# Splitting the mixers' and output projections' fp32 weights into high and low parts in four pieces instead of one or two

## The chip, the core and the metric

The kernel runs on one core of a Trainium2 chip. The metric is the device time of one execution in microseconds. The kernel is profiled once beside the timed runs; every row below is from that one execution.

## What is computed

The reference is one inference step of a two-layer streaming encoder for a prompt of 1024 tokens and a sample chunk of 64 tokens that share all weights. Model width is 1024, the feed-forward width 2816.

```
h = rmsnorm(x, norm_g[l, 0]) * (1.0 + sc1) + sh1
layer 0: retention (4 heads) || differential attention (4 heads):  h @ w_in_ab ... concat @ w_out_ab
layer 1: band attention (8 heads) || Mamba-2 SSD (8 heads):        h @ w_in_cd ... concat @ w_out_cd
x = x + g1 * out
h = rmsnorm(x, norm_g[l, 1]) * (1.0 + sc2) + sh2
u = h @ w_up[l]; a, g = u[:2816], u[2816:]
x = x + g2 * ((a * gelu(causal_dwconv(g))) @ w_down[l])
```

sc, sh and g come from the conditioning vector c (`silu(c) @ w_mod + b_mod`). The output is the final norm of x and all new caches and states, in fp32.

## The kernel before

All matrix products of the trunk are made in fp32r from two operands each: a high part `hi` (a copy rounded to fp32r) and a low part `lo = raw - hi`. A product is three matmuls: hi·hi, hi·lo and lo·hi. Activations are stored features-by-tokens in three token chunks of 384 columns (the third has 320), each as a hi and a lo tile.

**Weights.** A weight group is 256 output columns of a projection for all eight 128-row blocks k of the contraction, so a tile of 128 x 2048 fp32. `load_raw` (L185) or `load_two_raw` (L914) issues its DMA from SyncE's queue into `raw`, a pool of two buffers. `split_w` (L191) then takes `whi` and `wlo`, pools of two buffers each, and splits: ScalarE casts `raw` to `whi` (L198), and GpSimd (in the page's terms POOL) subtracts `whi` from `raw` into `wlo` (L199). The whole tile is one cast and one subtraction, unless the caller sets `urgent`: then there are two halves, the first subtracted by VectorE (DVE), the second by POOL. `urgent` is set in three places: the first query-key group of layer 0 (L1078), the first B/C group of layer 1 (L1706) and the first z group of layer 1 (L1783). 40 tiles go through `split_w`: the projections of the mixers (`load_two`, `load_cols`), the two output projections (L491, L1628, L2165) and the last pair of `w_down` rows of each layer (`load_rows`, L206). The up projection and most of `w_down` have a splitter of their own, `split` (L594, its cast is L595, its subtraction L596), which always works in pieces of 512 or 544 columns.

**Stages.** Layer 0 begins with the modulation and the first norm, then retention head by head (`core_ret`), with the projections of the next head woven between (`proj_ret`); then differential attention head by head (`diff_attention`), again with the next head's projection as filler; then the output projection, the feed-forward's up part in a Strassen-like form (`ffn_up`, L648) and its down part (`ffn_down`, L804). Layer 1 begins inside the end of `ffn_down` (`to_layer1`), goes through `project_z`, `project_x` and the state-space scan (`scan_group`) and band attention (`band_attention`), and ends as layer 0 does.

**What sets the order.** The five engines each run their own instruction list in order. The program is written as Python generators that are woven together, and a scheduler of the framework then orders each engine's list once more when the kernel is built. So an edit of one helper can shift neighbouring instructions of all engines.

Names that the prediction uses: `post` is the convolved SSD projection and `tt` its tanh, multiplied into it by DVE at L160 (`stt` is a helper, so all its calls have the line L160); `zt` is the gated z; `st` the SSD state, scaled on POOL (L1934) and added to on DVE (L1935); `t` stands for scan work tiles, which DVE subtracts `cum` from at L1911; `qj` holds attention queries as hi and lo parts (L1358); `pt` is the transposed probabilities; `cf` a row's factor in differential attention; `dg` a diagonal for the norm; `macc` the modulation's sums.

Of the kernel before, what the change touches and what calls it, by code (L numbers as in the profile page):

```python
# [142 lines left out]
def build(ctx, tc, A, O, stop=None):  # L143
    nc = tc.nc
    V, S, G, T = nc.vector, nc.scalar, nc.gpsimd, nc.tensor
# [45 lines left out]
    def split_w(raw, sz, urgent=False):  # L191
        hi = wsp.tile([P, WU], F32R, tag="whi", name="whi")
        lo = wsp.tile([P, WU], F32R, tag="wlo", name="wlo")
        n = 2 if urgent else 1
        for i in range(n):
            eng = V if urgent and i == 0 else G
            sl = slice(sz * i // n, sz * (i + 1) // n)
            S.copy(hi[:, sl], raw[:, sl])  # L198
            eng.tensor_tensor(out=lo[:, sl], in0=raw[:, sl], in1=hi[:, sl].bitcast(F32), op=ALU.subtract)  # L199
        return hi, lo  # L200

    def load_cols(w, c0, n=256, urgent=False):
        hi, lo = split_w(load_raw(w_src(w, c0, n), KT, n), KT * n, urgent)
        return [t[:, :KT * n].rearrange("p (k n) -> p k n", n=n) for t in (hi, lo)]

    def load_rows(w, r0):  # L206
        src = w[r0:r0 + 256, :].rearrange("(k p) n -> p k n", p=P)
        hi, lo = split_w(load_raw(src, 2, D), 2 * D)
        return [t[:, :2 * D].rearrange("p (k n) -> p k n", n=D) for t in (hi, lo)]
# [714 lines left out]
    def split_two(raw, urgent=False):  # L924
        hi, lo = split_w(raw, 2048, urgent)
        return [t[:, :2048].rearrange("p (k n) -> p k n", n=256) for t in (hi, lo)]
# [792 lines left out]
    class Modulation:  # L1719

        gen, n, every = None, 0, 1
# [517 lines left out]
```

## Time and profile before

| what | value |
|---|---|
| median of 3 runs | 2973.62 us (2972.55 to 2975.34) |
| the profiled execution's own time | 2973.83 us |
| its span, first to last instruction | 2972.1 us |
| mean granted TensorE clock | 0.979 of full speed |
| PE busy | 2804.1 us, 94% of the span |
| DVE busy | 1954.3 us, 66% |
| ACT busy | 1296.3 us, 44% |
| POOL busy | 787.3 us, 26% |

PE is TensorE's matmuls, ACT is ScalarE. An engine counts as busy from the start of an instruction to its end, also while the instruction stands still because something else holds what it needs; DVE's share must be read with that in mind. Windows of the page show PE at nine tenths or more in the feed-forward stages, and at seven or eight tenths in the start, late in each attention part, and where layer 1 begins.

### The profile page before, as it was taken

The numbers are of one execution on the slowest core, as the hardware profiler recorded it, in microseconds if no ns is written. First come the engines' busy times: TensorE is split into PE (matmuls) and PEld (weight loads), VectorE is DVE, ScalarE is ACT, GpSimd is POOL, SyncE is SP. The second block draws the span as 40 slices with busy tenths as digits, with TensorE's granted clock in tenths as the row PEclk, the third lists the DMA queues.
The fourth block names the chain that finished last, engine by engine and source line by source line (L and its number), as shares of the span: only waits on it lengthen the run. The fifth ranks groups of instructions, "written<-read, shape, count | busy, mean of one in ns | idle before, by whom it ended". The sixth has DMA issues, their size and how long they took to land.

```text
span 2972.1 us, 51195 instructions
## 1 busy us (share of the span) xinstructions
PE 2804.1 (94%) x19418; PEld 2707.4 (91%) x19418; DVE 1954.3 (66%) x4095; ACT 1296.3 (44%) x2938; POOL 787.3 (26%) x842
## 2 busy tenths in 40 slices
PE   7999999889999999999988999997999999999998
PEld 4999998779899999999988998986998999999997
DVE  5788766654788666587876675456268888764544
ACT  4221265644535444555552335556255454334111
POOL 4332222222255444412342352111100000004131
PEclk9999999889999999999989999999999999999999
DMA  7444421135544333553422331113344533235221
GB/s 241 139 131 142 126 62 60 46 98 159 158 130 137 91 101 96 183 173 128 138 82 74 86 98 50 52 55 93 99 132 144 153 101 102 71 98 184 90 81 61
DMA packets 351069, 330.53 MB, mean 111 GB/s; under 512 B 24898, under 2 KB 307047, under 8 KB 350823
## 3 DMA queue, kind: packets, MB, share of 16 engines
q1 hardware_dynamic: 350823, 327.26, 35.7%
q8 instruction: 153, 2.51, 0.4%
q14 instruction: 93, 0.76, 0.1%
HBM read 248.46 MB, written 78.73 MB: 110 GB/s over the span
## 4 chain that ended last, share of the span: by engine, by line
PE 47%; DVE 9%; DMA 6%; ACT 4%; issue 2%; POOL 1%; SPq 0%; DVEq 0%; ACTq 0%; POOLq 0%
PE dps L804 10%; PE pa L648 7%; PE pe L648 6%; PE pb L648 6%; DMA mh<-in_w_mod 3%; PE py L648 3%; PE qkps L231 3%; PE pvps L2110 2%; DMA raw<-in_w_up 2%; DVE macc L455 1%; ACT mh L453 1%; PE ops L231 1%; PE xps L231 1%; DVE wlo L596 1%; PE ptps L1316 1%
## 5 line engine op out<-in xcount | busy, mean ns | idle before, releaser
L804 PE MATMUL dps<-y,whi 128*128 128x384 f32 (+1 forms) x2112 | 518.8, 330 | 5.9 <-DVE sthi L160 4.2
L804 PEld LDWEIGHTS dps<-y,whi 128*128 128x128 f32 x2112 | 376.0, 189 | 7.2 <-DVE sthi L160 4.7
L595 ACT CAST whi<-raw 128x512 fp32r<-128x512 f32 x328 | 194.7, 617 | 372.4 <-PE pb L648 95.0
L804 PE MATMUL dps<-y,wlo 128*128 128x384 f32 (+1 forms) x1056 | 347.1, 330 | 0.0
L199 POOL TENSOR_TENSOR wlo<-raw,whi 128x2048 fp32r<-128x2048 f32 (+2 forms) x40 | 180.7, 4518 | 373.5 <-ACT whi L198 290.3
L160 DVE SCALAR_TENSOR_TENSOR x<-dps,modT,x 128x384 f32<-128x384 f32 (+1 forms) x320 | 149.4, 495 | 110.7 <-PE dps L804 110.1
L596 POOL TENSOR_TENSOR wlo<-raw,whi 128x512 fp32r<-128x512 f32 x116 | 162.1, 1402 | 208.1 <-ACT whi L595 203.1
L648 PE MATMUL pe<-row,whi 128*128 128x272 f32 x1056 | 205.9, 288 | 0.0
L804 PEld LDWEIGHTS dps<-y,wlo 128*128 128x128 f32 x1056 | 199.7, 189 | 0.0
L596 POOL TENSOR_TENSOR y<-y 128x544 fp32r<-128x544 f32 x88 | 133.0, 1543 | 250.4 <-ACT y L595 250.4
L453 ACT ACTIVATE mh<-mh,cact 128x256 f32<-128x256 f32 x336 | 145.8, 498 | 120.9 <-DMA mh<-in_w_mod 105.8
L455 DVE TENSOR_TENSOR macc<-macc,mh 128x512 f32<-128x512 f32 x168 | 142.7, 849 | 76.9 <-ACT mh L453 64.9
L596 DVE TENSOR_TENSOR wlo<-raw,whi 128x512 fp32r<-128x512 f32 x212 | 148.4, 718 | 64.1 <-ACT whi L595 63.4
L648 PE MATMUL pa<-row,whi 128*128 128x272 f32 x896 | 174.7, 292 | 10.3 <-ACT gs L669 10.3
L231 PE MATMUL qkps<-hhi,whi 128*128 128x384 f32 (+1 forms) x528 | 178.6, 342 | 3.3 <-DVE q L1383 2.0
L231 PE MATMUL qkps<-hlo,whi 128*128 128x384 f32 (+1 forms) x528 | 173.5, 332 | 0.0
L648 PEld LDWEIGHTS pe<-row,whi 128*128 128x128 f32 x1056 | 165.9, 188 | 0.0
L648 PE MATMUL pb<-bt,whi 128*128 128x272 f32 x816 | 156.8, 288 | 1.1 <-DVE u L717 1.1
L648 PE MATMUL pa<-bt,whi 128*128 128x272 f32 x768 | 151.0, 292 | 5.0 <-DVE row L160 3.1
L648 PEld LDWEIGHTS pa<-row,whi 128*128 128x128 f32 x896 | 143.1, 192 | 11.0 <-ACT gs L669 11.0
L648 PE MATMUL pe<-row,wlo 128*128 128x272 f32 x528 | 152.4, 289 | 0.0
L648 PE MATMUL py<-bt,whi 128*128 128x272 f32 x704 | 136.1, 290 | 4.0 <-ACT whi L595 2.4
(462 smaller groups left out, 8077.2 us busy)
## 6 DMA issues: line engine op xcount, KB each, us to landing
raw<-in_w_up SPq DMA_DIRECT2D x104, 512.0 KB
mh<-in_w_mod SPq DMA_DIRECT2D x96, 256.0 KB
yd<-e SPq DMA_DIRECT2D x88, 272.0 KB
y<-yd SPq DMA_DIRECT2D x44, 544.0 KB
raw<-in_w_down SPq DMA_DIRECT2D x22, 1024.0 KB
mq<-in_w_mod SPq DMA_DIRECT2D x64, 256.0 KB
raw<-in_w_in_ab SPq DMA_DIRECT2D x24, 512.0 KB
xr<-xspill SPq DMA_DIRECT2D x32, 193.0 KB
```

Of the source, the lines that this page charges most:

```text
L160: V.scalar_tensor_tensor(out=out, in0=in0, scalar=scalar, in1=in1, op0=op0, op1=op1, **kw)
L199: eng.tensor_tensor(out=lo[:, sl], in0=raw[:, sl], in1=hi[:, sl].bitcast(F32), op=ALU.subtract)
L231: T.matmul(out=ps[:, b:n], lhsT=lt, rhs=rh, start=(i == 0), stop=(i == len(mms) - 1))
L453: S.activation(out=pr[:, s, :], in_=rv[:, j - j0, :], func=AF.Copy, scale=cact[:, j, s:s + 1])
L455: V.tensor_add(acc, acc, pr)
L595: S.copy(hi, src)
L596: eng.tensor_tensor(out=lo, in0=src, in1=hi.bitcast(F32), op=ALU.subtract)
L648: T.matmul(out=ps[t], lhsT=lt, rhs=rh, start=(first and i == 0), stop=(i == len(mms) - 1), skip_group_check=not first)
L804: T.matmul(out=ps[:, :n], lhsT=lt, rhs=rh, start=(i == 0), stop=(i == len(mms) - 1))
L1316: T.transpose(ps[:kk, P * (b - b0):P * (b - b0 + 1)], e[:, P * b:P * b + kk], ident)
L2110: T.matmul(out=ps[:, :P], lhsT=pts[m][:kk, b, :], rhs=vv[:kk, :], start=(b == 0), stop=(b == nb - 1))
```

## The change

`split_w` works in four pieces, always: a 2048-column tile becomes four casts of 512 columns on ACT and four subtractions of 512 columns on POOL, piece by piece. With `urgent`, DVE subtracts the first two pieces and POOL the last two, so the columns of each of the two engines stay what they were. The z group has 2112 columns, so pieces of 528.

```diff
     def split_w(raw, sz, urgent=False):
         hi = wsp.tile([P, WU], F32R, tag="whi", name="whi")
         lo = wsp.tile([P, WU], F32R, tag="wlo", name="wlo")
-        n = 2 if urgent else 1
+        n = 4
         for i in range(n):
-            eng = V if urgent and i == 0 else G
+            eng = V if urgent and i < 2 else G
             sl = slice(sz * i // n, sz * (i + 1) // n)
             S.copy(hi[:, sl], raw[:, sl])
             eng.tensor_tensor(out=lo[:, sl], in0=raw[:, sl], in1=hi[:, sl].bitcast(F32), op=ALU.subtract)
```

Neither the number of matmuls nor a DMA changes. The scheduler's order does, in places. Two of them matter below.

The first is DVE at the start of layer 1, in `project_x`, where the tanh `tt` is multiplied into `post` while a z weight tile is split. Before:

```order
1834 L160 SCALAR_TENSOR_TENSOR post<-tt,post 128x384
1835 L160 SCALAR_TENSOR_TENSOR post<-acc_16682,pT_83,post 128x383
1836 L160 SCALAR_TENSOR_TENSOR post<-hist,pT_83,post 128x1
1837 L1858 COPY hist<-acc_16682 128x1
1838 L160 SCALAR_TENSOR_TENSOR post<-tt,post 128x384
1839 L160 SCALAR_TENSOR_TENSOR post<-acc_16683,pT_83,post 128x256
1840 L160 SCALAR_TENSOR_TENSOR post<-tt,post 128x384
1841 L160 SCALAR_TENSOR_TENSOR post<-acc_16683,pT_83,post 128x256
1842 L1791 TENSOR_TENSOR dtt<-zps,dtb 128x8
```

With the change:

```order
1846 L160 SCALAR_TENSOR_TENSOR post<-hist,pT_83,post 128x1
1847 L1858 COPY hist<-acc_16810 128x1
1848 L160 SCALAR_TENSOR_TENSOR post<-tt,post 128x384
1849 L160 SCALAR_TENSOR_TENSOR post<-acc_16811,pT_83,post 128x256
1850 L160 SCALAR_TENSOR_TENSOR post<-tt,post 128x384
1851 L1791 TENSOR_TENSOR dtt<-zps,dtb 128x8
1852 L160 SCALAR_TENSOR_TENSOR post<-acc_16811,pT_83,post 128x256
1853 L160 SCALAR_TENSOR_TENSOR post<-tt,post 128x384
```

The first of the three `tt` multiplications has moved down to the other two, because on ACT its tanh now stands behind the four casts.

The second is POOL late in the second half of the scan (`scan_group`), around the split of a weight group of band attention. Before:

```order
524 L1907 TENSOR_TENSOR t_18911<-t_18911,wl 128x256
525 L1943 TENSOR_TENSOR t_18824<-t_18824,t_18823 128x256
526 L1947 TENSOR_TENSOR t_18823<-t_18823 128x256
527 L1934 TENSOR_TENSOR st<-st,elast 128x256
528 L199 TENSOR_TENSOR wlo<-raw,whi 128x2048
529 L1950 TENSOR_SCALAR ss<-ss 128x1
```

With the change:

```order
528 L1907 TENSOR_TENSOR t_19073<-t_19073,wl 128x256
529 L199 TENSOR_TENSOR wlo<-raw,whi 128x512 x2
530 L1943 TENSOR_TENSOR t_18986<-t_18986,t_18985 128x256
531 L199 TENSOR_TENSOR wlo<-raw,whi 128x512 x2
532 L1934 TENSOR_TENSOR st<-st,elast 128x256
533 L1947 TENSOR_TENSOR t_18985<-t_18985 128x256
```

The state's scaling (L1934) stood ahead of the split and now stands behind all four pieces.

## Rows read from the trace of the kernel before

**Rows 1.** The page: busy time of the engines, and the chain that ended last by engine

```profile
PE 2804.1 (94%) x19418; PEld 2707.4 (91%) x19418; DVE 1954.3 (66%) x4095; ACT 1296.3 (44%) x2938; POOL 787.3 (26%) x842
...
PE 47%; DVE 9%; DMA 6%; ACT 4%; issue 2%; POOL 1%; SPq 0%; DVEq 0%; ACTq 0%; POOLq 0%
```

**Rows 2.** Who waited for line L198, the cast (us, times)

```profile
  PEld acc L216: 0.4, 1
```

**Rows 3.** Timeline at layer 1's start, POOL, DVE, PE (start us, us, what, idle)

```profile
1559.70 4.61 POOL L199 TENSOR_TENSOR wlo<-raw,whi 128x2048 fp32r<-128x2048 f32 x1 [6.92 <-ACT whi L198]
...
1560.08 4.64 DVE L160 SCALAR_TENSOR_TENSOR post<-tt,post 128x384 f32<-128x384 f32 x1 [2.73 <-ACT tt L1866]
...
1565.04 0.54 DVE L160 SCALAR_TENSOR_TENSOR post<-tt,post 128x384 f32<-128x384 f32 x1
...
1567.76 0.36 PE L247 MATMUL zps<-whi,hhi 128*128 128x264 f32 x1 [3.08 <-DVE zt L160]
```

**Rows 4.** Timeline of PE: idle behind other L199 splits, first group (last column: idle)

```profile
70.55 0.22 PE L1018 MATMUL mpt<-ident,mrow 2*128 2x2 f32 x1 [1.43 <-DVE mrow L1015]
...
100.52 0.39 PE L239 MATMUL vgps<-whi,hhi 128*128 128x256 f32 x1 [1.48 <-DVE rt L1172]
...
515.85 0.48 PE L1364 MATMUL sps<-ks,qj 128*128 128x512 f32 x1 [1.20 <-DVE mx L1304]
...
1664.27 0.36 PE L247 MATMUL zps<-whi,hhi 128*128 128x256 f32 x1 [1.24 <-DVE dco L1862]
```

**Rows 5.** The same, second group, with the DVE instruction that stood still

```profile
561.52 2.09 DVE L160 SCALAR_TENSOR_TENSOR cf<-sums,nlam,rr 128x1 f32<-128x1 f32 x1
...
565.71 0.50 PE L1364 MATMUL sps<-kcv,qj 128*128 128x512 f32 x1 [2.58 <-DVE kcv L1324]
...
1620.14 3.87 DVE L160 SCALAR_TENSOR_TENSOR post<-tt,post 128x320 f32<-128x320 f32 x1
...
1625.98 0.41 PE L231 MATMUL xps<-hhi,whi 128*128 128x386 f32 x1 [3.38 <-DVE post L1860]
...
2013.02 4.27 DVE L1358 TENSOR_TENSOR qj<-q,qj 64x128 fp32r<-64x128 f32 x1
...
2018.06 1.21 PE L2110 MATMUL pvps<-v,pt 128*128 128x128 f32 x8 [3.61 <-DVE pt L1318]
```

**Rows 6.** Groups by line and shape, POOL and ACT (busy us, mean ns; idle before)

```profile
L199 POOL TENSOR_TENSOR wlo<-raw,whi 128x2048 fp32r<-128x2048 f32 x37 | 172.5, 4663 | 372.7 <-ACT whi L198 289.6 <-PE ptps L1316 42.6 <-DVE x L160 16.6
L596 POOL TENSOR_TENSOR wlo<-raw,whi 128x512 fp32r<-128x512 f32 x116 | 162.1, 1402 | 208.1 <-ACT whi L595 203.1 <-DVE u L712 3.4 <-PE pe L648 1.5
...
L595 ACT CAST whi<-raw 128x512 fp32r<-128x512 f32 x328 | 194.7, 617 | 372.4 <-PE pb L648 95.0 <-PE dps L804 76.1 <-PE pa L648 62.9
...
L198 ACT CAST whi<-raw 128x2048 fp32r<-128x2048 f32 x37 | 70.6, 1908 | 106.4 <-PE dps L804 40.8 <-PE ops L217 30.8 <-issue 19.3
```

**Rows 7.** Timeline in layer 0's up projection, POOL and DVE, pieces of 512

```profile
830.10 1.27 POOL L596 TENSOR_TENSOR wlo<-s,whi 128x512 fp32r<-128x512 f32 x1
831.34 1.76 POOL L596 TENSOR_TENSOR wlo<-raw,whi 128x512 fp32r<-128x512 f32 x1
...
830.37 1.58 DVE L160 SCALAR_TENSOR_TENSOR e<-g,pT,e 128x543 f32<-128x543 f32 x1
...
831.99 1.69 DVE L160 SCALAR_TENSOR_TENSOR e<-g,pT,e 128x542 f32<-128x542 f32 x1
```

**Rows 8.** Timeline late in the scan: ACT, POOL, DVE and PE around a split

```profile
1763.35 1.93 ACT L198 CAST whi<-raw 128x2048 fp32r<-128x2048 f32 x1
...
1764.10 0.74 POOL L1943 TENSOR_TENSOR t<-t,t 128x256 f32<-128x256 f32 x1 [0.98 <-DVE t L1942]
...
1766.07 0.61 POOL L1934 TENSOR_TENSOR st<-st,elast 128x256 f32<-128x256 f32 x1
...
1771.77 0.41 DVE L1935 TENSOR_TENSOR st<-st,pst 128x256 f32<-128x256 f32 x1
...
1772.23 0.49 PE L1909 MATMUL pcb<-post 128*128 128x128 f32 x2 [3.63 <-DVE st L1935]
```

## The prediction

> **What bounds the kernel now.** I read the page's busy times first. PE is busy for 2804.1 of 2972.1 us and holds 47% of the chain that ended last, DVE 9%, ACT 4%, POOL 1% [rows 1]. The change adds and takes no matmul, so it can only act on the 168 us in which PE stands still. Next I asked who waits for the split. The cast L198 is waited for on PE's side for 0.4 us in all [rows 2]; the subtraction L199 appears in no such row. So the plain reading of the change, that a weight tile is ready sooner, is worth at most those 0.4 us.
>
> Then I laid the timelines of POOL, DVE and PE beside each other wherever an L199 ran. A pattern repeats. At 1559.70 POOL starts the subtraction of 2048 columns; it ends at 1564.31. At 1560.08 DVE starts `post<-tt,post`, both operands in SBUF, and needs 4.64 us; the same form takes 0.54 us at 1565.04 [rows 3]. DVE's end, 1564.72, is POOL's end plus 0.4 us: DVE stood still for the whole rest of POOL's instruction. PE then ran dry for 3.08 us behind DVE's queue. I count nine places where PE's idle time was over 1 us and such a block stood ahead of its releaser (a few more, smaller or less plain, I leave out): 3.08 us [rows 3]; 1.43, 1.48, 1.20 and 1.24 [rows 4]; 2.58, 3.38 and 3.61 [rows 5]; 3.63 [rows 8]. Together that is 21.63 us of PE idle time. The lever of this change is thus not the weight but the length of POOL's instruction.
>
> **Does a split of POOL's work let DVE through?** The trace of before shows it in the up projection, where the subtraction already comes in pieces of 512. POOL's piece runs from 830.10 to 831.37; a DVE operation that started at 830.37 takes 1.58 us and ends at 831.95. POOL's next piece is issued at 831.34 and takes 1.76 instead of 1.27 us; the next DVE operation starts at 831.99 and takes 1.69 us [rows 7]. They take turns: between two pieces that stand back to back, DVE gets one operation through. So a DVE operation waits for the rest of one piece. I take 1.40 us for it, the mean of that group of 116, which holds some waiting of its own; alone it is 1.27 [rows 6, 7]. Today's price is the mean 4.66 us [rows 6].
>
> **The terms.**
> - Four places with idle times of 1.43, 1.48, 1.20 and 1.24 us [rows 4]: a block of up to 4.66 us becomes 1.40, which is 3.26 less, more than any of them. All of it goes: 5.35 us. Below: nothing, if DVE meets several pieces.
> - `cf` at 561.52 stood for 2.09 us [rows 5], the tail of a split. At most 1.40 is left: 0.69 us of the 2.58.
> - `post<-tt,post` at 1620.14: 3.87, less 0.54 of its own work, less 1.40: 1.93 us of the 3.38 [rows 5].
> - `qj` at 2013.02: 4.27, less at most 0.54 of work, less 1.40: 2.33 us of the 3.61 [rows 5].
> - Layer 1's start [rows 3]: the block is 4.64 less 0.54, so 4.10 us. In the new DVE order three such multiplications stand together, where one was blocked; each may wait 1.40, so 4.20. But POOL starts after the first cast of 512 (617 ns) instead of one of 2048 (1908 ns) [rows 6], 1.29 us earlier. 4.10 - 4.20 + 1.29 = 1.19 us of the 3.08.
> - Late in the scan [rows 8]: the state's scaling L1934 now stands behind all four pieces. From the cast's start: 1763.35 + 0.62 + 4 x 1.40 + 0.74 (L1943) + 0.61 (L1934) = 1770.92. DVE's addition to the state began at 1771.77, so 0.85 us of the 3.63 is won. Bounds: 3.63, and a loss of about 1 if L1943 delays the second pair of pieces.
>
> Sum: 5.35 + 0.69 + 1.93 + 2.33 + 1.19 + 0.85 = 12.34 us.
>
> **What it costs.** ACT: four casts take 4 x 617 - 1908 = 560 ns more than one, 37 times: 20.7 us. POOL: 4 x 1402 - 4663 = 945 ns more, 37 times: 35.0 us, part of which is waiting for DVE [rows 6]. The work that hides both is PE's own; of the chain ACT has 4% and POOL 1% [rows 1]. I charge those shares: 0.8 + 0.4 = 1.2 us. Without the cover, ACT's 20.7 us would stand whole. The three urgent splits keep their engines and columns; DVE and POOL already alternate there, so I put them at nothing. Apart from the two places above, about 390 of some 18,600 matmuls stand in another place in PE's list, most of them in the last heads of the attentions and in the scan; no row prices this, its sign is open, and I take zero, with 5 us either way for the range.
>
> 12.34 - 1.2 = 11.1 us. The profiled execution took 2973.83 us (span 2972.1), 0.2 above the median of the three runs. 2973.83 - 11.1 = 2962.7, and against the median **2962.5 us**.
>
> **Rivals.**
> *More comes back.* The 1.40 us is a bound, and a DVE operation on average meets a piece that has run for a while; the time saved ahead of DVE also reaches places whose idle time I didn't list. If all 21.63 us go: 2952.0, with 2 us beyond for unlisted ones. Against: rows 7, where both DVE operations waited over a microsecond. Chance 0.10.
>
> *PE's time comes back as the next wait.* At about half of the nine places PE's releaser is several DVE operations behind the blocked one (`zt` behind `post` [rows 3], `kcv` behind `cf`, the last step of `post` behind its product [rows 5]), and what replaces the block can be the next step of the same chain, or a POOL step now behind four pieces. For it: the scan's new POOL order. Against: the releaser moves forward with the block. Worth about the four short gaps less the reordering: 2968 to 2976, at its middle 2972. Chance 0.17. That the change doesn't do what it says (the weights earlier) belongs here too: it would leave 2973.2.
>
> *POOL keeps the shared path through all four pieces.* The pieces stand back to back in POOL's list. If a waiting DVE operation doesn't get between them, its block is 4 x 1.40 = 5.60 us instead of 4.66: 0.94 more at each of the nine places, 8.5 us, and ACT's longer casts with it, 1.2: 2983. It decides where DVE's next operation depends on the one before it and so comes a moment late, as at 831.99 [rows 7]: there POOL's piece went first. With one such operation the change wins, from about four in a row it loses. For it: the three multiplications of layer 1's start. Against: the first operation in rows 7 did get in. Chance 0.10.
>
> *ACT's longer casts stand whole on the path.* Then nothing is won and 20.7 us are added: 2973.6 + 20.7 = 2994. For it: 617 ns for a quarter of what takes 1908 [rows 6]. Against: ACT is busy for 44% and has 4% of the chain [rows 1]. It decides only where PE waits on ACT. Chance 0.02. The Trainium skill has a rule that speaks for this case: "VectorE: DVE Perf Modes", section "The TRN2 errata", says that a VectorE or ScalarE operation reading SBUF pays a fixed latency per instruction, so that many small tiles pay it many times, and advises tiles of 512 elements or more; the pieces sit just at that edge. The trace agrees with it on ACT, in the 560 ns above.
>
> **How the numbers follow.** A measurement of this kernel tells 0.2% from no change, 5.9 us: faster means under 2967.7, slower over 2979.6. The forecast's own case has 0.61, with a range from 2954 to 2968: above by the doubt on the four short places (5.35 us), below by blocks shorter than 1.40. Faster: 0.61 + 0.10 = 0.71. Same: the wait that returns, 0.17. Slower: 0.10 + 0.02 = 0.12. The range runs from 2950 (all nine places and 2 us) to 2976 (the top of the returning wait); it leaves out the slower cases and a few hundredths below.
>
> **What would show it.** L199 on POOL has some 148 pieces of 512 with a mean near 1.4 us and no DVE operation beside it stands for over 2 us; `qj`, `post<-tt,post` and `cf` beside a split are 1 to 2 us long. The PE idle times in rows 4 are gone, that behind `qj` near 1.3 us, the one behind the state's addition still at 2 to 3 us. DVE's busy time falls by 20 us or more; ACT's rises by about 20. PE's busy time stays at 2804 within 5. I am wrong if DVE operations stand through several pieces, if PE's idle times reappear behind POOL (L1934, L301) or ACT, or if the last attention heads, where only the order changed, move by more than 5 us.

## The result, and the profile after

The change takes 2939.18 us (median of four runs, 2937.28 to 2940.24) against 2974.14 us for the kernel before in the same comparison: a ratio of 0.9882, with a 95% interval of 0.9866 to 0.9897. That is 35 us less. The direction was forecast; the size, 11 us, was three times too small, and the time lies below the range.

The page of the change: busy times, and the chain by engine [rows 1 before] (PEld is TensorE's loading of weights).

```profile
PE 2790.2 (95%) x19418; PEld 2696.8 (92%) x19418; DVE 1926.1 (66%) x4098; ACT 1310.0 (45%) x3055; POOL 813.4 (28%) x956
...
PE 37%; DVE 4%; DMA 3%; ACT 2%; issue 1%; SPq 0%; POOL 0%; DVEq 0%; POOLq 0%; ACTq 0%
```

The span fell from 2972.1 to 2935.5 us, by 36.6. It splits in two. PE's idle time (span less busy) went from 168.0 to 145.3 us, 22.7 less. PE's busy time fell by 13.9 us, though PE executes the same 19,418 matmuls.

The groups by line and shape, POOL, then ACT (busy us, mean ns) [rows 6 before]:

```profile
L199 POOL TENSOR_TENSOR wlo<-raw,whi 128x512 fp32r<-128x512 f32 x152 | 201.6, 1357 | 372.7 <-ACT whi L198 241.4 <-PE ops L219 71.5 <-PE ptps L1316 44.2
L596 POOL TENSOR_TENSOR wlo<-raw,whi 128x512 fp32r<-128x512 f32 x116 | 162.2, 1404 | 205.9 <-ACT whi L595 204.4 <-PE pe L648 1.5
...
L198 ACT CAST whi<-raw 128x512 fp32r<-128x512 f32 x156 | 85.3, 619 | 110.6 <-PE dps L804 42.8 <-PE ops L217 29.1 <-issue 18.6
```

POOL's pieces last 1.36 us, as assumed (1.40). ACT's busy time rose by 13.7 us, not 20.7: casts that stand back to back overlap in part (156 casts of 0.619 us would be 96.6 us, and the busy time of the group is 85.3).

Layer 1's start, POOL, DVE, PE [rows 3 before]:

```profile
1544.75 5.68 POOL L199 TENSOR_TENSOR wlo<-raw,whi 128x512 fp32r<-128x512 f32 x4 [7.21 <-ACT whi L198]
...
1546.12 1.59 DVE L160 SCALAR_TENSOR_TENSOR post<-tt,post 128x384 f32<-128x384 f32 x1 [4.48 <-ACT tt L1866]
...
1548.03 1.25 DVE L160 SCALAR_TENSOR_TENSOR post<-tt,post 128x384 f32<-128x384 f32 x1
...
1549.67 1.17 DVE L160 SCALAR_TENSOR_TENSOR post<-tt,post 128x384 f32<-128x384 f32 x1
...
1552.56 0.36 PE L247 MATMUL zps<-whi,hhi 128*128 128x264 f32 x1 [2.12 <-DVE zt L160]
```

The block of 4.64 us has become three of 1.2 to 1.6 us, one piece of POOL each, and PE's idle time went from 3.08 to 2.12 us. The same matmul in the other places of the forecast, PE's timeline [rows 4, 5 before]:

```profile
99.75 0.58 PE L239 MATMUL vgps<-whi,hhi 128*128 128x256 f32 x1 [3.55 <-DVE rt L1172]
...
562.12 0.63 PE L1364 MATMUL sps<-kcv,qj 128*128 128x512 f32 x1 [1.89 <-DVE kcv L1324]
...
1604.14 0.41 PE L231 MATMUL xps<-hhi,whi 128*128 128x386 f32 x1 [0.63 <-DVE dco L1862]
...
1636.75 0.36 PE L247 MATMUL zps<-whi,hhi 128*128 128x256 f32 x1 [0.24 <-DVE dco L1862]
...
1986.24 0.94 PE L2110 MATMUL pvps<-v,pt 128*128 128x128 f32 x6 [0.25 <-DVE pt L1318]
```

The other three (`mpt`, `sps` after 510 us, and the state in the scan) have no idle time left. Of the 21.63 us of the nine places, 8.68 remain: 3.55 + 1.89 + 0.63 + 0.24 + 0.25 + 2.12. So the nine places gave 12.95 us where 12.34 were forecast. The rest of the 36.6, 23.7 us, came from elsewhere: 9.75 us of idle time (22.7 less 12.95) and the 13.9 us of busy time.

Where it came from is seen when both traces are cut at the same matmuls: start, differential attention of layer 0, up projection, down projection, layer 1's start with the scan, band attention, and the second feed-forward. Before, then the change (stretch, its length, PE busy, PEld, DVE, ACT, POOL, granted clock, DMA):

```profile
378.50:737.30 358.80, 327.51 (x2049) 306.61 (x2048) 212.44 (x585) 189.35 (x491) 91.95 (x141) 0.96 0.29 85
...
1228.00:1513.40 285.40, 274.34 (x1656) 270.75 (x1654) 210.47 (x370) 157.86 (x340) 86.74 (x64) 0.99 0.48 153
1513.40:1821.30 307.90, 279.48 (x1832) 270.10 (x1831) 203.95 (x489) 115.66 (x281) 123.38 (x159) 0.95 0.29 84
1821.30:2197.40 376.10, 347.22 (x2313) 324.70 (x2312) 181.69 (x467) 189.33 (x533) 50.15 (x43) 0.98 0.26 76
```

```profile
379.50:731.30 351.80, 321.91 (x2049) 302.99 (x2047) 208.24 (x585) 191.30 (x510) 97.65 (x162) 0.97 0.29 87
...
1221.70:1498.60 276.90, 271.91 (x1658) 269.39 (x1656) 203.13 (x370) 159.81 (x350) 89.55 (x73) 1.00 0.48 158
1498.60:1792.80 294.20, 274.90 (x1831) 265.82 (x1829) 187.08 (x490) 118.81 (x307) 130.28 (x186) 0.96 0.30 88
1792.80:2164.50 371.70, 345.63 (x2312) 323.39 (x2312) 175.67 (x467) 191.61 (x552) 52.66 (x59) 0.98 0.26 76
```

These four stretches are 7.0, 8.5, 13.7 and 4.4 us shorter. PE's idle time (length less busy) fell from 11.1 to 5.0 us in the down projection, from 28.4 to 19.3 in layer 1's start and scan, and from 28.9 to 26.1 in band attention. In differential attention it fell only from 31.3 to 29.9, so most of the 7.0 us there is PE's busy time. The forecast had no place in the down projection at all.

**What was left out.** The down projection carries the modulation of layer 1 as side work: ACT scales (`mh`), DVE adds up (`macc`), PE turns the sum (`mps`, L409). Before, three splits of `w_down` rows lie there (three tiles per layer, not a pair). One of them, POOL and DVE before:

```profile
1439.47 4.64 POOL L199 TENSOR_TENSOR wlo<-raw,whi 128x2048 fp32r<-128x2048 f32 x1 [23.88 <-ACT whi L198]
...
1438.48 1.66 DVE L160 SCALAR_TENSOR_TENSOR x<-dps,modT,x 128x384 f32<-128x384 f32 x3
1440.23 4.42 DVE L455 TENSOR_TENSOR macc<-macc,mh 128x512 f32<-128x512 f32 x1
```

`macc`, with both inputs in SBUF, stands until POOL's end. The accumulation of `dps` ahead of it, one input in PSUM, takes 0.55 us each: the seven of its 384-column form that lie beside a whole subtraction in this trace take 0.62 us from start to end, the 153 others 0.61. Two of PE's waits for `macc` behind such a block, before:

```profile
1416.99 0.66 PE L409 MATMUL mps<-ident,macc 128*128 128x128 f32 x4 [1.42 <-DVE macc L455]
...
1455.73 0.66 PE L409 MATMUL mps<-ident,macc 128*128 128x128 f32 x4 [1.16 <-DVE macc L455]
```

All of them, total us, times, longest, before and after:

```profile
PE mps L409 <- DVE macc L455: 9.4, 7, 2.6
```

```profile
PE mps L409 <- DVE macc L455: 4.0, 4, 2.2
```

Not all of that fall belongs to the splits. The first of the three starts at 1410.98 us; the four waits behind it make up 4.2 of the 9.4 us, and 0.6 is left of them. The other 5.2 us, which became 3.4, stand where no `w_down` rows are split.

Another place left out lies in `project_z`: the first of the steps that make `spt` stood behind a split, and PE waited 2.10 us for its end, some dozen DVE instructions later. POOL, DVE and PE before:

```profile
1592.44 4.61 POOL L199 TENSOR_TENSOR wlo<-raw,whi 128x2048 fp32r<-128x2048 f32 x1 [28.13 <-ACT whi L198]
...
1593.01 4.26 DVE L1804 TENSOR_SCALAR spt<-spt 128x72 f32<-128x72 f32 x1
...
1601.02 0.42 PE L231 MATMUL xps<-hhi,whi 128*128 128x386 f32 x1 [2.10 <-DVE spt L160]
```

In the change PE has no idle time at that matmul.

**The clock.** The mean granted clock went from 0.979 to 0.982. The time lost to the lower level is thus about (1 - 0.979) x 2972.1 = 62.4 us before and (1 - 0.982) x 2935.5 = 52.8 us after (each to 1.5 us, from rounding): some 10 of the 13.9 us that PE was busy for less. The four largest waits of layer 1 show the connection: six microseconds from each of the matmuls that had waited 3.08, 3.38, 3.63 and 3.61 us [rows 3, 5, 8], and the six from the same places in the change, where 2.12, 0.63, 0.00 and 0.25 were waited (the clock is the third number from the end):

```profile
1567.76:1573.76 6.00, 6.00 (x37) 6.00 (x38) 4.26 (x17) 2.33 (x6) 0.00 (x0) 0.72 0.72 220
1625.98:1631.98 6.00, 6.00 (x25) 6.00 (x26) 5.93 (x20) 1.37 (x3) 0.70 (x2) 0.72 0.61 205
1772.23:1778.23 6.00, 6.00 (x28) 5.82 (x29) 2.61 (x7) 0.95 (x4) 3.49 (x6) 0.72 0.30 80
2018.06:2024.06 6.00, 6.00 (x35) 5.83 (x36) 2.69 (x7) 1.44 (x6) 0.00 (x0) 0.72 0.54 145
```

```profile
1552.56:1558.56 6.00, 6.00 (x49) 6.00 (x50) 5.65 (x23) 2.47 (x7) 0.00 (x0) 1.00 0.62 210
1604.14:1610.14 6.00, 6.00 (x34) 5.95 (x35) 5.93 (x20) 2.83 (x8) 1.67 (x5) 1.00 0.75 236
1744.23:1750.23 6.00, 4.15 (x27) 3.34 (x26) 1.72 (x6) 1.14 (x4) 2.78 (x5) 0.99 0.99 275
1986.24:1992.24 6.00, 5.25 (x40) 4.71 (x40) 3.96 (x9) 3.48 (x10) 2.99 (x3) 1.00 0.35 114
```

At a mean of 0.72, part of each stretch ran at 1.2 GHz; behind the 3.38 us PE began 25 matmuls instead of 34. By estimate these four cost (1 - 0.72) x 6 us each, 6.7 us in all.

### The profile page after: what moved, and what is told of

Its sections match the earlier page's. It is cut to its first block, busy times and chain, and to the rows that moved or that the text cites. A ratio compares the mean times of both kernels' runs of the same rounds, so it can differ in the third digit from the quotient of the medians.

```text
span 2935.5 us, 51435 instructions
## 1 busy us (share of the span) xinstructions
PE 2790.2 (95%) x19418; PEld 2696.8 (92%) x19418; DVE 1926.1 (66%) x4098; ACT 1310.0 (45%) x3055; POOL 813.4 (28%) x956
## 5 line engine op out<-in xcount | busy, mean ns | idle before, releaser
L199 POOL TENSOR_TENSOR wlo<-raw,whi 128x512 fp32r<-128x512 f32 (+1 forms) x154 | 205.1, 1363 | 372.7 <-ACT whi L198 241.4
L455 DVE TENSOR_TENSOR macc<-macc,mh 128x512 f32<-128x512 f32 x168 | 134.1, 798 | 68.4 <-ACT mh L453 60.5
```

The source lines that it names most:

```text
L455: V.tensor_add(acc, acc, pr)
```

## The experiments

Theory A: the lever is POOL's instruction, which holds DVE up; its length counts. Rivals: B, the weights' first pieces reach PE sooner; C, the scheduler's other lists; P, the moment at which POOL starts; L, PE waits for `wlo`. All results together. A ratio is against runs of the kernel before that were made beside the kernel of its row; their medians lie between 2971.6 and 2974.5 us, so small differences are read from ratios, not from medians. PE's idle time is span less busy of the profiled execution:

| kernel | median us | ratio (95%) | PE idle us | PE busy us | clock |
|---|---|---|---|---|---|
| before | 2974.14 | | 168.0 | 2804.1 | 0.979 |
| before, again (one run) | 2981.97 | | 166.4 | 2813.8 | 0.975 |
| urgent splits alone | 2976.26 | 1.0009 (0.9996 to 1.0022) | 171.8 | 2799.3 | 0.980 |
| layer 0's mixers alone | 2975.29 | 1.0006 (0.9997 to 1.0015) | 169.5 | 2808.7 | 0.978 |
| 4 casts, 1 subtraction | 2971.10 | 0.9989 (0.9978 to 1.0) | 166.7 | 2801.7 | 0.979 |
| `w_down` rows alone | 2969.60 | 0.9991 (0.998 to 1.0002) | 163.2 | 2801.6 | 0.981 |
| layer 1's mixers alone | 2957.71 | 0.9944 (0.9924 to 0.9964) | 159.4 | 2796.0 | 0.982 |
| 1 cast, 4 subtractions | 2955.26 | 0.9939 (0.9923 to 0.9955) | 159.6 | 2792.4 | 0.982 |
| 2 pieces | 2953.29 | 0.9933 (0.9908 to 0.9958) | 151.7 | 2801.1 | 0.979 |
| layer 1 and rows | 2951.04 | 0.9936 (0.9918 to 0.9953) | 148.5 | 2798.3 | 0.981 |
| 8 pieces | 2947.47 | 0.9909 (0.9883 to 0.9936) | 148.1 | 2797.9 | 0.981 |
| 4 pieces, urgent as before | 2944.62 | 0.9908 (0.9879 to 0.9937) | 148.5 | 2794.2 | 0.981 |
| whole cast in layer 0 | 2940.14 | 0.9894 (0.9879 to 0.9909) | 148.9 | 2787.8 | 0.984 |
| the change, 4 pieces | 2939.18 | 0.9882 (0.9866 to 0.9897) | 145.3 | 2790.2 | 0.982 |
| 8 pieces on DVE | 2937.40 | 0.9878 (0.986 to 0.9896) | 148.2 | 2787.4 | 0.983 |
| 1 piece on DVE | 2933.33 | 0.9858 (0.9831 to 0.9885) | 143.3 | 2791.2 | 0.982 |
| 4 pieces on DVE | 2927.09 | 0.9848 (0.9833 to 0.9862) | 141.2 | 2784.6 | 0.986 |

**Cast or subtraction?** First the loop was split in two, so that each count could be set by itself (m casts, n subtractions; urgent as before where the count is one):

```diff
+        m, n = (2, 4) if urgent else (1, 4)
+        for i in range(m):
+            S.copy(hi[:, sl], raw[:, sl])
+        for i in range(n):
+            eng.tensor_tensor(out=lo[:, sl], in0=raw[:, sl], in1=hi[:, sl].bitcast(F32), op=ALU.subtract)
```

> The subtraction in four pieces, the cast whole as before (two halves where urgent). Theory A (POOL's long instruction holds up DVE, the length of that instruction is the lever): the gain stays whole, 2930 to 2948 us, and no DVE instruction beside an L199 piece stands for over 2 us. Theory B (the first pieces of a weight reach PE sooner because the casts are short): the gain goes, 2968 to 2978. Theory C (the gain is the scheduler's other order of the lists, which this edit shifts in another way again): no tie to either kernel, anywhere from 2935 to 2985.

The other way round, (4, 2) if urgent else (4, 1):

> The casts in four pieces, the subtraction one whole instruction of 2048 columns as before. Theory A: the blocks of 4.6 us on DVE are back, so no gain: 2968 to 2985, 2974 plus part of ACT's 20.7 us of longer casts. Theory B: the gain stays, below 2950. Theory C: anywhere from 2935 to 2985.

Four casts before a whole subtraction win next to nothing (2971 us), so B falls. Four subtractions behind a whole cast win 19 us, half: more than B allows and less than A expected. One reason is visible in the scan [rows 8 before]. With the whole cast, the four additions of `cum` stand back to back beside the four pieces (DVE, POOL, PE; lines are shifted by 2):

```profile
1745.30 4.88 DVE L1913 TENSOR_SCALAR t<-t,cum 128x128 f32<-128x128 f32 x4 [1.52 <-DMA t<-cumd]
...
1745.13 4.97 POOL L201 TENSOR_TENSOR wlo<-raw,whi 128x512 fp32r<-128x512 f32 x4
...
1750.57 0.49 PE L1911 MATMUL pcb<-post 128*128 128x128 f32 x2 [3.47 <-DVE st L1937]
```

Each addition lets one piece go first, so the four together take as long as they did beside the whole instruction (5.02 us before), and PE's 3.63 us stay at 3.47. In the change POOL's other steps stand between the pieces, and this wait is gone. (So the order of the lists counts at this place.) Late in band attention this run also has a `pvps` that waits 3.27 us, where 0.78 stood before; the run with layer 1 alone, below, has 3.28 there and the change 0.21.

The whole subtraction behind four casts is the instructive one in differential attention. DVE, before and with four casts:

```profile
510.36 4.94 DVE L160 SCALAR_TENSOR_TENSOR e<-e,cf 128x512 f32<-128x512 f32 x1
```

```profile
510.57 0.75 DVE L160 SCALAR_TENSOR_TENSOR e<-e,cf 128x512 f32<-128x512 f32 x1
...
511.63 4.42 DVE L1360 TENSOR_TENSOR qj<-q,qj 64x256 fp32r<-64x256 f32 x1
```

POOL starts half a microsecond later (510.63 against 510.15), `e<-e,cf` gets through ahead of it, and the block falls on `qj`. PE's idle time of 1.20 us at `sps` is gone without any shorter piece, but it has moved rather than ended: PE now waits at `kops`. PE before and with four casts:

```profile
517.84 0.55 PE L1397 MATMUL kops<-ident,kx 128*128 128x128 f32 x3 [0.52 <-DVE pt L1318]
```

```profile
517.86 0.55 PE L1399 MATMUL kops<-ident,kx 128*128 128x128 f32 x3 [1.78 <-DVE pt L1320]
```

Which instruction a block hits decides where PE waits.

**Where?** Four pieces for some of the weights only:

```diff
+    FOUR = ('in_w_in_cd', 'in_w_out_cd')
...
+        n = 2 if urgent else 4 if four else 1
```

with layer 0's two names instead, or with the `w_down` rows.

> Four pieces for the weights of layer 0's mixers and its output projection alone; w_down's rows, layer 1 and the urgent splits as before. Theory A, from where the two traces part: the lead at the end of layer 0's output projection was 6 us, so 2965 to 2971, and the trace after 740 us runs parallel to that of before. Theory C: no such sum; the lead at the end of layer 0's attention differs from 6 us by more than 4, or the rest does not run parallel.

> Four pieces for the weights of layer 1's mixers and its output projection alone; the rest as before. Theory A: the block at 1463 in the end of the down projection (2 us), the scan (12 to 15 us) and the band attention (4 us) win: 2951 to 2957, and up to 1440 us the trace is that of before. Together with the run of layer 0 alone and some 3 to 9 us of the w_down rows this should add up to the 35 us. Theory C: the parts do not add up, by more than 10 us.

> Four pieces for the six tiles of w_down rows alone (three per layer); all the rest as before, and the list of PE nearly so. Theory A: the three blocks of macc in layer 0's down projection end, 5.9 us (the steps of the change between 1410 and 1480 us: 1.64, 1.10, 0.94, 1.29, 0.97), nothing in layer 1, where no macc is summed: 2966 to 2970. Theory P (luck of the moment): no gain there, or gains at other places: 2971 to 2979.

> Four pieces for layer 1's weights and the w_down rows, two halves where urgent, layer 0's mixers and output projection whole. Theory A: the run of layer 1 alone (16.6 us) and the three macc blocks (5.9 us) add up: 22.5 us, 2948 to 2955. If layer 0's pieces are needed for what comes later: 2957 or more.

Layer 1 alone gives 17 us, with the rows 19 by the ratio and 21 by the medians, close to what A expected (2957.7 is 0.7 us over its range, 2951.0 within it). The rows alone came out at 2969.6 us, within the 2966 to 2970 of A, but the interval (0.998 to 1.0002) doesn't exclude no change; the profile does better: PE's idle time in that run is 163.2 us, 4.8 less than before, and its waits for `macc` fell from 9.4 to 4.8 us. Layer 0's mixers give nothing on their own (2975, where A expected 2965 to 2971): PE's idle time is 169.5 us. That fits the forecast's four places in layer 0, which had 6.69 us before and keep 5.44 in the change.

By the measure written down before, this is C's sign: layer 0, layer 1 and the rows alone give -1, 17 and 2 us, 18 of the 35, and so fall short by more than 10. Idle time narrows it down. With layer 1 and the rows together it falls by 19.5 us (148.5), though by 8.6 and 4.8 in the two runs apart, and it is the same 148.5 us when layer 0's pieces are added (four pieces, urgent as before); the change has 145.3. So layer 0's pieces take away no idle time that these runs can see, and of the 12 to 16 us between the run with layer 1 and rows and the change, only 3.2 are idle time. The others are PE's busy time, which one execution doesn't resolve (below). Why layer 1 and the rows together take away 6 us more idle time than apart is not shown.

That it is all the order of the lists, as C has it, is contradicted by the four large waits of layer 1, PE's idle time in us ahead of the same matmul:

| kernel | `zps` [rows 3] | `xps` [rows 5] | state [rows 8] | `pvps` [rows 5] |
|---|---|---|---|---|
| before | 3.08 | 3.38 | 3.63 | 3.61 |
| before, again | 3.08 | 3.40 | 3.64 | 3.61 |
| rows alone | 3.08 | 3.40 | 3.63 | 3.61 |
| 4 casts, 1 subtraction | 3.83 | 3.67 | 0.00 | 3.49 |
| 1 cast, 4 subtractions | 1.60 | 0.11 | 3.47 | 0.37 |
| layer 1 alone | 0.70 | 0.65 | 0.00 | 0.25 |
| 2 pieces | 2.45 | 1.54 | 0.00 | 0.00 |
| the change | 2.12 | 0.63 | 0.00 | 0.25 |
| 4 pieces on DVE | 0.69 | 0.98 | 0.00 | 0.69 |

At `xps` and `pvps` the wait follows the pieces through all the lists, and so does the one of 2.10 us for `spt`: it stands in every kernel whose layer 1 has whole subtractions on POOL, is 1.11 with four pieces behind a whole cast, 0.37 with two pieces of both, and gone in the change. `zps` and the state follow the order as well: the state's wait went with four casts ahead of a whole subtraction too. The `pvps` row of that run, and of the one with pieces in layer 1 and the rows:

```profile
2014.62 1.08 PE L2112 MATMUL pvps<-v,pt 128*128 128x128 f32 x7 [3.49 <-DVE pt L1320]
```

```profile
1994.42 0.82 PE L2112 MATMUL pvps<-v,pt 128*128 128x128 f32 x5 [0.25 <-DVE pt L1320]
```

**How short, and the urgent ones?**

```diff
+        n = 2
```

> Two pieces of 1024 columns always (the urgent splits as before). Theory A (the gain follows the length of POOL's instruction): about half of the gain in layer 1 from 1570 to 2020 us, in all 2948 to 2962. Theory P (part of the gain, the 7 us in layer 0's differential attention and 4 to 9 us in its down projection, comes from POOL starting at another moment, whatever the length: it was there with the whole subtraction behind four casts too): that part is here as well, in full, 6 to 8 us in the differential attention.

> Eight pieces of 256 columns, half of them on DVE where urgent. Theory A: a DVE instruction waits for 0.75 us at most, so the places of layer 1 win what they win with four pieces or a little more; ACT pays some 0.5 us more per weight; 2932 to 2943. If the gain is over at four pieces, because a wait of 1.3 us is already hidden: 2937 to 2943. Theory P: the gains in layer 0 change by some us either way.

> Four pieces, but the three urgent splits in two halves as before. Theory A and P: these three are not where the time came from, so within 4 us of the change, 2935 to 2944. If the handovers at the start of the layers (urgent halves of 1024 columns, on DVE 3.1 and 3.5 us beside POOL) matter: 2944 to 2955.

> Only the three urgent splits in four pieces, the 37 others whole. Theory A and P: 2969 to 2979, no change. If the handovers matter: 2955 to 2968, with the gain before 110 us and between 1510 and 1575 us.

The length of POOL's instruction is the dose: 4.66, 2.46, 1.36 and 0.79 us give 2974, 2953, 2939 and 2947 us, and 168.0, 151.7, 145.3 and 148.1 us of idle time. Two pieces fell in A's range. Eight pieces, at 2947, lie above every range expected for them (2932 to 2943); the intervals of four and eight overlap, so no gain and no clear loss is seen beyond four. Of P's fixed share of 6 to 8 us in differential attention two pieces showed only 2 (that stretch, cut as above, was 2.3 us shorter), so P's share isn't fixed either. Nor does the length of this stretch say much: with the rows alone, whose first split comes some 670 us behind its end, it is 4.1 us shorter too, with only 0.2 us less idle time. The three urgent splits alone win nothing. Leaving them out of the change gave 2944.6, on the edge between the two expectations, with overlapping intervals: not told apart.

**Whole casts for layer 0 only.**

```diff
+        m, n = (2 if urgent else 1) if whole else 4, 4
```

> Four subtractions everywhere, the cast whole for layer 0's mixers and output projection and in four for the rest. Where layer 0 is as in the run with the cast whole, it saves 4.4 us before 378 us (the idle of 3.55 us at the first vgps is gone) and the same 8 us in the differential attention; the rest as the change: 2931 to 2938. If these 4.4 us are luck of the moment: 2938 to 2944.

2940.1: the same as the change, not told apart from it. The wait at the first `vgps` did fall, to 0.35 us, but that gain did not carry to the end.

**The same pieces without POOL.**

```diff
-            eng = V if urgent and i < 2 else G
+            eng = V
```

> All four subtractions on DVE, none on POOL: DVE gets some 110 instructions of 0.7 us more in its list, 75 to 100 us of work, but no L199 on POOL holds it up. Theory A: a DVE instruction waits for one piece of 0.7 us at a time instead of 4.6, so most of the gain is there: 2938 to 2955. If DVE's own load is what binds (65% busy), the pieces stand on the path: 2965 to 3000.

> One cast, one subtraction of 2048 columns, on DVE. Theory A (what holds DVE up is POOL's instruction on the path that both share; it is long because POOL is slow): no block, but each subtraction holds DVE for some 2.6 us of its own work, as long as POOL's of 1024 columns: 2943 to 2960. Theory L (the length of POOL's instruction counts because PE waits for wlo): DVE's is shorter than POOL's 4.6 us, all of the gain: below 2935.

> Eight pieces of 256 columns, all on DVE. Theory A: a piece of 0.4 us instead of 0.7, already hidden at most places; ACT's and DVE's fixed cost per instruction speaks against it: 2925 to 2934, no better than four pieces on DVE. If pieces still bind at four: 2915 to 2923.

Four pieces on DVE take 2927.1 us, better than both kernels and below A's range of 2938 to 2955. Eight take 2937.4, above both ranges expected (2915 to 2934): there, too, more pieces win nothing. One whole subtraction, at 2933.3, is not told apart from four pieces on DVE, nor from the change: the intervals overlap. The groups on DVE, four pieces, then one (busy us, mean ns):

```profile
L198 DVE TENSOR_TENSOR wlo<-raw,whi 128x512 fp32r<-128x512 f32 x156 | 105.3, 716 | 13.9 <-ACT whi L197 13.8
```

```profile
L198 DVE TENSOR_TENSOR wlo<-raw,whi 128x2048 fp32r<-128x2048 f32 x39 | 90.6, 2323 | 26.6 <-ACT whi L197 26.2
```

Their pages:

```profile
PE 2784.6 (95%) x19418; PEld 2691.6 (92%) x19418; DVE 1975.3 (68%) x4252; ACT 1308.7 (45%) x3055; POOL 613.7 (21%) x802
```

```profile
PE 2791.2 (95%) x19418; PEld 2699.5 (92%) x19418; DVE 1962.1 (67%) x4132; ACT 1297.7 (44%) x2935; POOL 621.5 (21%) x802
```

With one whole subtraction on DVE, L199 keeps DVE busy for 92.9 us (90.6, and 2.3 for the z group) instead of 7.9 before (the urgent halves), 85 us more, and its busy time rose by only 7.8 us (1954.3 to 1962.1): some 77 us of standing still are gone. In the change DVE's busy time fell by 28 us alone, so by this reckoning most of the standing still is still there, while PE's idle time (145.3 against 143.3 us) is nearly the same. A's number for the whole subtraction on DVE was wrong: it expected 2.3 us on DVE to cost what 2.46 us on POOL costs (2953 us), and 2933 were measured. The number is L's (just, the interval reaches past 2935), but not for L's reason: in none of these profiles does PE wait once for the subtraction of `split_w`, and in the change the last piece of `wlo` comes hardly earlier than the whole did (6.2 us from the first cast's start instead of 6.6, at the `w_down` tile at 1410 us). That DVE's own instruction is cheaper because the scheduler knows its length and orders DVE's list by it, and can't know a block, is an argument that no run here tests.

**How much is chance in one execution?** The kernel before, with no edit.

> The kernel before, unchanged, profiled once more, for the size of the chance in one profiled execution. Where a step stood in all kernels, also in those that hadn't touched the place (1.5 us at 650 us, 2.3 us at 1305 us), it should stand here too: theory of chance. If it doesn't, these steps come from the edits. The four places in layer 1 (3.1, 3.4, 3.6 and 3.6 us of idle time) should be as in the first profile within 0.3 us.

The four waits of layer 1 stood again to 0.02 us (table above). PE's idle time was 166.4 us against 168.0. But PE was busy for 9.7 us longer and the clock was 0.975. So, as far as one repeat tells, PE's idle time in all can be read from one execution to 2 us, and PE's busy time only to 10. Single places can move more: of the nine places, the first `vgps` stood at 2.33 us instead of 1.48 and the `zps` at 1664 us at 2.79 instead of 1.24, the other seven within 0.03. The steps at 650 and 1305 us stood as in the first profile, so they are not chance of one execution; since kernels that didn't touch those places lost them too, they hang on the moment. Steps of a single stage under some 5 us are therefore not explained here.

## Why the prediction was wrong in size

**Right.** The direction, and the mechanism: POOL's long instruction holds DVE up, and shorter pieces let DVE through. DVE's instructions that wait beside a piece last 1.1 to 1.8 us. One is over 2: `e<-e,cf` of 1024 columns at 559 us, 2.26 us, which takes 1.29 without a split beside it. The subtractions on POOL are 154 with a mean of 1.36 us; DVE's busy time fell by 28 us ("20 us or more").

**Right by luck.** The sum over the nine places, 12.95 us against 12.34, holds misses that cancel. The four short places gave 1.56 us instead of 5.35, since the first `vgps` waited 2.07 us longer. The state gave 3.63 instead of 0.85, `xps` and `pvps` 2.75 and 3.36 instead of 1.93 and 2.33, `zps` 0.96 instead of 1.19. `cf` came out to the hundredth (0.69 us), but not as reckoned: in the change `cf` isn't held up at all (0.32 us), and the block falls on the `e<-e,cf` behind it. And in the repeated profile of the kernel before, the nine places sum to 24.0 us instead of 21.63, so the 12.95 itself is good to some 2 us.

**What holds DVE up.** An instruction of DVE's stands until POOL's ends, if both of its inputs are in SBUF: `macc` stands 4.42 us, the form with an input in PSUM passes at 0.55. Two inputs aren't needed: the `tensor_scalar` forms `spt` and `t<-t,cum` stand too, 4.26 us and 4.88 for four. Who starts first goes first: half a microsecond at 510 us decides between `e<-e,cf` and `qj`. Back-to-back pieces and waiting DVE instructions alternate, one for one (4.88 us for the four of the run with the whole cast). The Trainium skill, "SBUF — State Buffer", section "Who interferes with whom", says that a DVE instruction with two SBUF inputs and a GpSimd instruction that reads SBUF need the same ports, that whoever comes first keeps them for the whole instruction, and that issue order decides. The traces agree: `macc` at 4.42 us for the first two parts, the half microsecond at 510 us for the third.

**The step that failed** is the list of places. "I count nine places where PE's idle time was over 1 us and such a block stood ahead of its releaser (a few more, smaller or less plain, I leave out)": what was left out gave 9.75 us net of PE's idle time (22.7 less 12.95), three quarters as much again. Not all of it was small: the wait for `spt` (2.10 us) and two of those for `macc` (1.42 and 1.16) were over the forecast's own limit of 1 us. The three `macc` blocks of the down projection are the largest part: cut at the same matmuls, PE's idle time between 1400 and 1480 us, 4.9 us before, is gone in the change and in the same change without the urgent splits, and 3.5 of it is gone with the rows alone. The rival "more comes back" had 2 us for all unlisted places.

**A second step that failed:** "PE's busy time stays at 2804 within 5." It fell by 13.9 us, some 10 of them the clock. The forecast put this at nothing because no matmul is added or taken: "so it can only act on the 168 us in which PE stands still". It is this step that took the time out of the range: the 22.7 us of idle time alone would have left 2951 us, just inside it. Each of the long idle times was priced at its own length; the slower matmuls behind it weren't priced at all, and behind the four large waits of layer 1 these cost 6.7 us by the estimate above (the new wait of 2.79 us, below, has its own: the clock stands at 0.51 in the six microseconds from its end, 2.9 us). The repeated profile says that 10 us of clock can also be chance in one execution. All timed runs point the same way as the single ones: the granted clock has a mean of 0.979 over 53 runs of the kernel before (0.975 to 0.983) and of 0.982 over the four of the change (0.981 and 0.982), some 7 us by estimate. Among the profiled executions it is 0.981 to 0.986 in the kernels with 141 to 149 us of idle time, 0.979 and twice 0.982 in the three with 152 to 160, and 0.975 to 0.981 in those with 163 to 172. The exact size isn't settled.

**Terms that missed within the sum.** At the first `vgps` 1.48 us was to vanish and 3.55 stand there: in DVE's new list sixteen instructions of `fcor`, `pT`, `dcor` and `macc`, 3.4 us in all, stand ahead of two `rt`, of which PE waits for the second; before, most of them stood behind it (DVE in the change, the first of the sixteen and that `rt`):

```profile
95.25 1.25 DVE L380 TENSOR_TENSOR fcor<-pT,pT 128x22 f32<-128x22 f32 x1
...
99.21 0.49 DVE L1172 TENSOR_TENSOR rt<-acc,csin 64x322 f32<-64x322 f32 x1
```

The state in the scan was put at 0.85 us of 3.63, and all of it went; but DVE then comes to a load that isn't there yet, and PE idles 2.79 us at a place that had no wait before. DVE and PE in the change:

```profile
1749.78 0.87 DVE L1911 TENSOR_SCALAR t<-t,cum 128x128 f32<-128x128 f32 x4 [3.43 <-DMA t<-cumd]
...
1751.17 0.69 PE L231 MATMUL qkps<-hhi,whi 128*128 128x384 f32 x1 [2.79 <-DVE q L1383]
```

That is the rival "the time comes back as the next wait", true for this one place (the same matmul waits 2.7 to 3.2 us in four other runs with four pieces in layer 1, and not at all in either profile of before). The forecast took zero for matmuls that move in PE's list and, apart from its two places, had no term for a new order of DVE's list, which made the first of these. The cost terms (1.2 us) were too small to matter.

**The other rivals.** That POOL keeps the shared path through all pieces isn't seen: no DVE instruction beside the change's pieces lasts longer than one piece and its own work. But its point of decision, four DVE instructions in a row, was met in the run with the whole cast, where nothing was won at the state. ACT's casts don't stand on the path: four casts with a whole subtraction are no slower than before.

## What to carry to other kernels

When an engine's instruction holds another engine up, list every instruction that stood beside it and follow each to its waiter, side work too; the list of nine places priced about half of the idle time that came back here, and none of the clock that came back with it. Shorten the holding instruction until shorter pieces win nothing more (here near 1.4 us), or better, give the work to the engine that was held up, if it has room: with one whole subtraction there, 85 us more work on DVE cost 8 us of its time, and the best kernel here has all four pieces on DVE, 2927.1 us (0.9848 of before, 0.9833 to 0.9862). Read idle time, not busy time, when one profiled execution is all there is.

## What the hardware showed that was not expected

A block is not priced by its length but by what it hits: half a microsecond of POOL's start moved a block of over 4 us from `e<-e,cf` to `qj`, and PE's wait from `sps` (1.20 us, gone) to `kops` (1.78 instead of 0.52). Each of the four waits of over 3 us in layer 1 was followed by six microseconds at a mean granted clock of 0.72; at the same places in the change, where the waits had shrunk, it was 0.99 to 1.00. And the same kernel, profiled twice, kept its idle time to 1.6 us (168.0 and 166.4), though single places moved by 0.9 and 1.6 us, while PE's busy time differed by 9.7 us at granted clocks of 0.979 and 0.975.
